# Token-major V for two head groups at a time: 512 columns per matmul, k blocks outermost, five PSUM banks open

## The chip, the cores and the metric

The kernel runs on one core of one Trainium2 chip. The metric is device time in microseconds (us). Five engines work side by side and wait for each other through semaphores: TensorE (PE, with its weight loads shown apart as PEld), VectorE (DVE), ScalarE (ACT), GpSimd (POOL) and SyncE (SP), which here does nothing but start DMAs. TensorE multiplies a stationary operand of 128 columns, which a weight load puts into the array, with a moving operand that streams past it, and writes sums into PSUM, eight banks of 128 x 512 fp32.

## The reference

One layer of a decoder: 512 prompt tokens and 64 sample tokens (8 sequences of 8) share all weights. All tokens are projected by one wide matrix; two of the three branches of the mixer have a "V" in it:

```python
(q_g, k_g, v_g, r_g, a_lr, u_pool, q_a, k_a, v_a,
 g_a, g_b, g_c) = jnp.split(xn @ w_in, _split_points(), axis=-1)
v_g = v_g.reshape(bsz, t_len, GLA_HEADS, GLA_DV)          # 4 heads x 256: gated linear attention
o_g, gla_new = gla_chunked(q_g, k_g, v_g, log_a, s0)
...
v_a = v_a.reshape(bsz, t_len, ATT_HEADS, ATT_HEAD_DIM)    # 12 heads x 64: dilated attention
for gi, (win, dil) in enumerate(ATT_GROUPS):              # (128,1), (512,4), (2048,16)
    hs = slice(gi * ATT_HEADS_PER_GROUP, (gi + 1) * ATT_HEADS_PER_GROUP)
    qh, kh, vh = q_a[:, :, hs], k_a[:, :, hs], v_a[:, :, hs]
```

A group of the dilated attention has 4 heads x 64 = 256 columns of V. In groups 1 and 2 a query reads keys 4 and 16 tokens apart, so the kernel holds the tokens of these two groups in strided order (token t, t+4, t+8, ...).

## The kernel before

Everything is fp32 in value. To multiply at TensorE's fast rate, each operand is split into a rounded high part and the rest (`xh`, `xl` for the normalised tokens; `wh`, `wl` for weights), and a product is three matmuls: high by high, low by high, high by low. A weight "chunk" is 1,024 fp32 per partition, loaded by one DMA of SP into one of three buffers `wr`; it is cut into two pieces of 512 by a copy on ACT (line 148, `wh`) and a subtraction on DVE (line 150, `wl`), each tag with four buffers. The list `chunks` fixes the order of loading; `fetch(i)` cuts chunks i and i+1 and loads i+2 and i+3.

Most projections are made by `gemm` (line 231): the weights are stationary, tokens are the moving operand in two parts of 256 to 320 columns, and the result has channels on partitions. V is needed with tokens on partitions, so `token_major` (lines 400 to 432, its matmuls on line 423) turns the roles round: a block of 128 tokens of `xh` or `xl` is stationary, and 256 columns of weights stream. It goes through the token blocks one after another (block 4, the 64 sample tokens packed as high and low parts into `xsp`, first; then 0, 1, 2, 3), for each through the eight blocks of k; blocks 2 and 3 are done in two halves of k. That is 4 x 8 x 3 + 8 x 2 = 112 matmuls. Blocks 0 and 1 share a bank. It is called seven times: for each of the four heads h of the gated linear attention (lines 535 to 538), and for the attention groups 2, 1, 0 (line 1011). For groups 2 and 1 the stationary block is `xh[:, n, t::4]`: 128 tokens that lie four fp32 apart.

PSUM has a pool `g` of three banks (`big`) and a pool of five (`small`, of which one bears the tag `h`). Evacuations: line 427 (ACT) and 428 (DVE) add the two halves of the sample block, 430 and 432 (ACT) copy the token blocks.

The order in which instructions stand on each engine is not that of the code: a scheduler builds it at compile time from its own estimate of durations, and pools decide when a buffer is free. On the chip each engine then runs its list strictly in order. So dense matmuls of `gemm` and V stand between the small steps of the two attentions, as filler for their waits. Steps that the prediction names: in the gated linear attention of head h the norm's sums (line 682), the transposes of `kp` (581), `kp` itself (POOL, 568 and 569), and the scans of the forget gate (DVE, 502 and 503); in the dilated attention, which runs one prompt unit and some steps of a sample unit in turn, the products with cached keys and values (910, 893, 898, 965; the cache arrives in four buffers `kv`), the softmax of a sample (819, 946, 948, 949), the values of the prompt (849, 857), the rescaling (1084, 1086) and the last transposes (1092). The gates `gc` (line 1101) are 384 dense matmuls that follow the attention in the code, and stand between its steps in the order; the last 24 of them are held until line 1092 has run.

Of the kernel before, what the change touches and what calls it, by code (L numbers as in the profile page):

```python
# [9 lines left out]
F32 = mybir.dt.float32  # L10
# [3 lines left out]
OP = mybir.AluOpType  # L14
# [6 lines left out]
NP = 512  # L21
# [12 lines left out]
C_Q, C_K, C_V, C_R, C_LR, C_U = 0, 512, 1024, 2048, 3072, 3088  # L34
C_QA, C_KA, C_VA, C_GA, C_GB, C_GC = 4112, 4880, 5648, 6416, 7440, 8464
# [69 lines left out]
def hybrid_step(ctx: ExitStack, tc: tile.TileContext, I, O, at_a, at_b):  # L105
    nc = tc.nc
    V, S, G, T = nc.vector, nc.scalar, nc.gpsimd, nc.tensor
# [8 lines left out]
    def big():  # L116
        return psg.tile([128, 512], F32, tag="g", name="g")
# [6 lines left out]
    def small():  # L124
        turn[0] += 1
        if turn[0] % 5 == 0 and not apart[0]:
            return held()
        return pss.tile([128, 512], F32, tag="s", name="s", bufs=4)
# [13 lines left out]
    chunks = []  # L142
# [51 lines left out]
    for b in range(8):  # L194
        for which in range(2):
            for g in (2, 1, 0):
                src = I[KEYS[g][which]][0, b].rearrange("t h e -> t (h e)")
# [14 lines left out]
    def plan(name, c0, cols=128, r0=0, kt=8, plain=True):  # L212
        chunks.append(Chunk(rows(name, c0, cols, r0, kt), kt, cols, plain))
        return len(chunks) - 1

    def fetch(i):
        for n in range(i, min(i + 2, len(chunks))):
            chunks[n].split()
        for n in range(i + 2, min(i + 4, len(chunks))):
            if chunks[n].plain:  # L220
                chunks[n].load()
# [51 lines left out]
    P = {}  # L273
    GROUPS = (2, 1, 0)
    for h in range(4):
        P["k", h] = [plan("w_in", C_K + 128 * h)]
        P["q", h] = [plan("w_in", C_Q + 128 * h)]
        P["v", h] = [plan("w_in", C_V + 256 * h, 256, r, 4) for r in (0, 4)]
        for d in range(2):
            P["r", 2 * h + d] = [plan("w_in", C_R + 256 * h + 128 * d)]  # L280
    def plan_u(n):
# [25 lines left out]
    for g in GROUPS:  # L307
        for p in range(2):
            P["qa", 2 * g + p] = [plan("w_in", C_QA + 256 * g + 128 * p)]
            P["ka", 2 * g + p] = [plan("w_in", C_KA + 256 * g + 128 * p)]  # L310
        P["va", g] = [plan("w_in", C_VA + 256 * g, 256, r, 4) for r in (0, 4)]
    for m in range(8):
        P["gc", m] = [plan("w_in", C_GC + 128 * m)]
    for m in range(8):
# [14 lines left out]
    xh = xpool.tile([128, 8, NT], F32R, tag="xh", name="xh")  # L329
    xl = xpool.tile([128, 8, NT], F32R, tag="xl", name="xl")  # L330
# [41 lines left out]
    for t in range(5):  # L372
        n = 128 if t < 4 else 64
# [26 lines left out]
    def token_major(ids, order, out_p, out_s, tmp, xsp):  # L400

        fetch(ids[0])
        fetch(ids[1])
        ps = {4: big(), 0: big()}
        ps[1] = ps[0]
        for ts, ns in (((4,), range(8)), ((0,), range(8)), ((1,), range(8)), ((2, 3), range(4)), ((2, 3), range(4, 8))):
            for t in ts:
                if t not in ps:
                    ps[t] = big()
                c = 256 if t == 1 else 0  # L410
                dst = ps[t][:, c:c + 256]
                sel = slice(128 * t, 128 * t + 128) if order == 1 else slice(t, NP, 4)
                for n in ns:
                    wh, wl = chunks[ids[n // 4]].wide(n % 4)
                    if t < 4:
                        lh, ll = xh[:, n, sel], xl[:, n, sel]
                        seq = ((lh, wh), (ll, wh), (lh, wl))
                    else:
                        seq = ((xsp[:, n, :], wh), (xsp[:, n, :], wl))
                    for j, (a, b) in enumerate(seq):  # L420
                        first = t == 2 and n == 4 and j == 0
                        with tc.issue_after(mm.ins) if first else nullcontext():
                            mm = T.matmul(dst, a, b, start=(n == 0 and j == 0), stop=(n == 7 and j == len(seq) - 1))  # L423
                if ns[-1] < 7:
                    continue
                if t == 4:
                    S.copy(tmp, ps[4][64:128, :256])
                    V.tensor_tensor(out_s, ps[4][:64, :256], tmp, op=OP.add)  # L428
                elif t == 1:
                    S.copy(out_p[:, 0:2].rearrange("p b c -> p (b c)"), ps[1])  # L430
                elif t > 1:
                    S.copy(out_p[:, t, :], dst)


    xs_cm, xs_pool = open_pool("xs", "left")
    xsp = packed_sample(xs_pool)
# [85 lines left out]
    for h in range(4):  # L522
# [5 lines left out]
        for nm, dst, sc in (("k", kT, 1.0), ("q", qT, 128.0 ** -0.5)):  # L528
            if h:
                gemm(P[nm, h], XH, XL, lambda ps, t0, t1: S.mul(dst[:, t0:t1], ps, sc))  # L530
            else:
                for x, ps, a, b in kq0:
                    if x == nm:
                        S.mul(dst[:, a:b], ps, sc)
        vt = gl.tile([128, 4, 256], F32, tag="vt", name="vt", bufs=2)
        vs = gl.tile([64, 256], F32, tag="vs", name="vs", bufs=2)
        vtmp = gl.tile([64, 256], F32, tag="vtmp", name="vtmp", bufs=1)
        token_major(P["v", h], 1, vt, vs, vtmp, xsp)
        nc.sync.dma_start(sg, I["state_gla"][0, :, h].rearrange("b k v -> k b v"))

        bp, bs = views(bb[h])
# [450 lines left out]
    for g in GROUPS:  # L992
        W = WIN[g]
        load_bias(g)
        qT = ap.tile([128, 2, NP], F32, tag="aq", name="aq", bufs=2)
        kT = ap.tile([128, 2, NP], F32, tag="ak", name="ak", bufs=2)
        vt = ap.tile([128, 4, 256], F32, tag="av", name="av", bufs=2)
        vtmp = ap.tile([64, 256], F32, tag="avt", name="avt", bufs=1)
        for p in range(2):
            for nm, dst, dsts, sc in (("qa", qT, qs, 0.125), ("ka", kT, ksn, 1.0)):  # L1000
                def evac(ps, t0, t1):
                    if g == 0:
                        S.mul(dst[:, p, t0:t0 + 256], ps[:, :256], sc)
                    else:
                        S.mul(dst[:, p, :].rearrange("p (r i) -> p r i", r=4)[:, :, t0 // 4:t0 // 4 + 64],
                              ps[:, :256].rearrange("p (i r) -> p r i", r=4), sc)
                    if t0:
                        S.mul(dsts[:, 2 * g + p, :], ps[:, 256:], sc)

                gemm(P[nm, 2 * g + p], XH, XL, evac, SPLIT)  # L1010
        token_major(P["va", g], 1 if g == 0 else 4, vt, vsn[g], vtmp, xsp)
        if g == 2:
            pt = small()
            for p in range(2):
                qd = sa.tile([128, 2, 64], F32, tag="qd", name="qd", bufs=1)
                for d in range(2):
                    V.tensor_copy(qd[:, d, :], qs[:, 4 + p, :])
                T.transpose(pt[:, 128 * p:128 * p + 128], qd.rearrange("p d n -> p (d n)"), ident)
            qhl = sa.tile([128, 256], F32R, tag="qhl", name="qhl")
            S.copy(qhl, pt[:, :256])  # L1020
            V.tensor_tensor(qhl[64:128], pt[64:128, :256], qhl[64:128].bitcast(F32), op=OP.subtract)
            sel = sa.tile([128, 64], F32R, tag="sel", name="sel")
            V.tensor_tensor(sel, ident[:, 0:64], ident[:, 64:128], op=OP.add)

        for _ in prompt_units(g, qT, kT, vt):
            for _ in range(STEPS[g]):
                next(samples, None)
        if g == 0:
            for _ in samples:
                pass  # L1030

        ko = sa.tile([128, 4, 256], F32, tag="kv", name="ko", bufs=4)
        for t in range(4):
            if g == 0 and t < 3:
                continue
            pk = small()
            for p in range(2):
                T.transpose(pk[:, 128 * p:128 * p + 128], kT[:, p, 128 * t:128 * t + 128], ident)
            S.copy(ko[:, t, :], pk[:, :256])
        kos = ap.tile([64, 256], F32, tag="avt", name="kos", bufs=1)  # L1040
        pk = small()
        for p in range(2):
            T.transpose(pk[:64, 128 * p:128 * p + 128], ksn[:, 2 * g + p, :], ident)
        S.copy(kos, pk[:64, :256])
        for n, tok, smp in ((K_OUT[g], ko, kos), (V_OUT[g], vt, vsn[g])):
            o = O[n][0, 0].rearrange("t h e -> t (h e)")
            if g == 0:
                nc.sync.dma_start(o, tok[:, 3, :])
            else:
                nc.sync.dma_start(o.rearrange("(i r) f -> i r f", r=4), tok)  # L1050
            for b in range(8):
                nc.sync.dma_start(O[n + 1][0, b].rearrange("t h e -> t (h e)")[W - 8:W], smp[8 * b:8 * b + 8, :])
        if g == 1:
            nc.sync.dma_start(scr.rearrange("(i r) c -> i r c", r=4), stp.rearrange("p r g m h -> p r (g m h)"))
            nc.sync.dma_start(nat[:, :, 1:3].rearrange("p t g m h -> p t (g m h)"), scr.rearrange("(t p) c -> p t c", p=128))
# [461 lines left out]
```

## Time and profile before

| what | before |
|---|---|
| time, median of 3 runs | 1308.93 us (1308.63 to 1310.06) |
| the profiled execution's own time | 1308.33 us |
| its span, first to last instruction | 1306.3 us |
| mean granted TensorE clock | 0.998 |
| matmuls on line 423, by the page's groups of 224 (prompt blocks) | 71.2, 71.1 and 70.8 us, 318, 318 and 316 ns each |
| first and last start of line 423 | 35.8 and 684.1 us |

A matmul's duration in the trace has a modelled end, and the next one starts before it is over; what a matmul costs the engine is therefore read from the distance between two starts. A timeline row gives start, duration, engine, line, operation, out<-in, sizes (stationary, then moving) and count; in brackets stands how long the engine was idle before it and who released it.

### The profile page before, as it was taken

To read this page: it belongs to the slowest core of one execution; us is meant where nothing else is said; L and a number is where in the kernel's file an instruction comes from. 1 tells how busy PE (TensorE), PEld (TensorE's weight loads), DVE (VectorE), ACT (ScalarE), POOL (GpSimd) and SP (SyncE) were. 2 spreads that over 40 slices of the span, in tenths; PEclk is the share of its full clock that TensorE was granted. 3 is DMA by queue.
4 is the path that set the end of the run, shared out by engine and by line. 5 is a ranking of instruction groups with operands and counts; after the bars stand their busy time and mean duration, and the time that the engine had idled before them with its cause. 6 is when DMAs were issued, how large, how long until landed. Compare 5 with 4: busy or idle time off the path is not lost.

```text
span 1306.3 us, 24224 instructions
## 1 busy us (share of the span) xinstructions
PE 1276.7 (98%) x9699; PEld 1226.0 (94%) x9699; DVE 685.9 (53%) x1294; ACT 572.0 (44%) x1262; POOL 250.0 (19%) x400
## 2 busy tenths in 40 slices
PE   8899999999999999999999999999999999999996
PEld 6899999999999999998988879999999999999996
DVE  5855554333462323172733357545897878873233
ACT  6654553544332222243543334444456656662333
POOL 4321212013420222041311101022231222200000
PEclk9999999999999999999999999999999999999999
DMA  7242432376483677355766432563556656544423
GB/s 221 66 125 62 146 113 74 98 232 192 154 257 93 216 239 245 110 168 174 219 195 211 141 103 78 161 216 114 161 151 151 141 132 146 125 113 141 137 77 117
DMA packets 225484, 196.39 MB, mean 150 GB/s; under 512 B 8444, under 2 KB 216937, under 8 KB 224596
## 3 DMA queue, kind: packets, MB, share of 16 engines
q1 hardware_dynamic: 218682, 142.28, 37.3%
q0 software_dynamic: 6688, 52.57, 13.3%
q8 instruction: 76, 1.25, 0.4%
q14 instruction: 36, 0.29, 0.1%
q10 hardware_dynamic: 2, 0.00, 0.0%
HBM read 175.52 MB, written 54.27 MB: 176 GB/s over the span
## 4 chain that ended last, share of the span: by engine, by line
PE 82%; issue 5%; DVE 5%; ACT 4%; DMA 3%; SPq 1%; POOL 0%; POOLq 0%; ACTq 0%; DVEq 0%
PE g L231 43%; PE g L1431 8%; PE g L423 7%; PE g L1274 6%; PE s L1274 3%; PE s L1431 2%; DMA wr<-wr 1%; DVE wl L150 1%; PE h L1274 1%; PE s L833 1%; PE s L231 1%; PE h L965 1%; PE s L910 1%; PE s L893 1%; ACT wh L148 1%
## 5 line engine op out<-in xcount | busy, mean ns | idle before, releaser
L150 DVE TENSOR_TENSOR wl<-wr,wh 128x512 fp32r<-128x512 f32 (+2 forms) x286 | 202.0, 709 | 324.2 <-ACT wh L148 318.2
L231 PE MATMUL g<-xh,wh 128*128 128x288 f32 (+2 forms) x1120 | 333.6, 298 | 3.1 <-DVE ae L1320 1.6
L231 PE MATMUL g<-xh,wl 128*128 128x288 f32 (+2 forms) x1120 | 333.9, 298 | 0.5 <-DVE wl L150 0.5
L231 PE MATMUL g<-xl,wh 128*128 128x288 f32 (+2 forms) x1120 | 332.1, 296 | 0.0
L148 ACT CAST wh<-wr 128x512 fp32r<-128x512 f32 (+2 forms) x290 | 174.9, 607 | 339.1 <-PE g L231 232.0
L231 PEld LDWEIGHTS g<-xh,wh 128*128 128x128 f32 x1120 | 211.1, 189 | 5.8 <-issue 2.5
L231 PEld LDWEIGHTS g<-xh,wl 128*128 128x128 f32 x1120 | 211.0, 188 | 2.8 <-issue 1.4
L231 PEld LDWEIGHTS g<-xl,wh 128*128 128x128 f32 x1120 | 211.0, 188 | 1.6 <-issue 1.3
L1234 DVE TENSOR_TENSOR wl<-wr,wh 128x512 fp32r<-128x512 f32 x119 | 81.2, 707 | 22.9 <-ACT wh L1233 22.6
L1233 ACT CAST wh<-wr 128x512 fp32r<-128x512 f32 x119 | 70.2, 619 | 46.3 <-DVE wr L1225 23.7
L423 PE MATMUL g<-wh,xh 128*128 128x256 f32 x224 | 71.2, 318 | 2.8 <-DVE vs L428 2.8
L1431 PE MATMUL g<-hh,wh 128*128 128x288 f32 (+2 forms) x286 | 71.3, 297 | 0.2 <-ACT hh L1245 0.2
L1431 PE MATMUL g<-hh,wl 128*128 128x288 f32 (+2 forms) x286 | 71.2, 297 | 0.0
L423 PE MATMUL g<-wh,xl 128*128 128x256 f32 x224 | 71.1, 318 | 0.0
L423 PE MATMUL g<-wl,xh 128*128 128x256 f32 x224 | 70.8, 316 | 0.0
L1431 PE MATMUL g<-hl,wh 128*128 128x288 f32 (+2 forms) x286 | 70.7, 296 | 0.0
L1274 PE MATMUL g<-xh_t,wh 128*128 128x288 f32 x204 | 60.6, 297 | 0.5 <-DVE h L1367 0.3
L1274 PE MATMUL g<-xh_t,wl 128*128 128x288 f32 x204 | 60.3, 296 | 0.0
L1274 PE MATMUL g<-xl_t,wh 128*128 128x288 f32 x204 | 59.9, 294 | 0.0
L423 PEld LDWEIGHTS g<-wh,xh 128*128 128x128 f32 x224 | 51.6, 230 | 4.2 <-DVE vs L428 3.0
L423 PEld LDWEIGHTS g<-wh,xl 128*128 128x128 f32 x224 | 51.6, 230 | 1.6 <-issue 1.6
L423 PEld LDWEIGHTS g<-wl,xh 128*128 128x128 f32 x224 | 51.7, 231 | 0.0
(520 smaller groups left out, 2984.6 us busy)
## 6 DMA issues: line engine op xcount, KB each, us to landing
wr<-in_w_in_dram SPq DMA_DIRECT2D x74, 512.0 KB
wr<-in_ffn_w_up_dram SPq DMA_DIRECT2D x44, 512.0 KB
out_dram<-in_cache_k_w_dram POOLq DMA_DIRECT2D x8, 2040.0 KB, 9.6
out_dram<-in_cache_v_w_dram POOLq DMA_DIRECT2D x8, 2040.0 KB, 9.7
kv<-in_cache_k_w_dram SPq DMA_DIRECT2D x26, 512.0 KB
kv<-in_cache_v_w_dram SPq DMA_DIRECT2D x26, 512.0 KB
wr<-wr POOLq DMA_DIRECT2D x34, 256.0 KB, 3.6
wr<-in_ffn_w_down_dram SPq DMA_DIRECT2D x18, 448.0 KB
```

The source lines that it names most:

```text
L148: S.copy(hi[:, :n], src)
L150: return hi, lo, E.tensor_tensor(lo[:, :n], src, hi[:, :n].bitcast(F32), op=OP.subtract)
L231: T.matmul(ps[:, :t1 - t0], a, b(n)[:, t0:t1], start=(n == 0 and j == 0), stop=(n == len(ks) - 1 and j == 2))
L423: mm = T.matmul(dst, a, b, start=(n == 0 and j == 0), stop=(n == 7 and j == len(seq) - 1))
L833: T.matmul(sps[hh][:, nk * n:nk * n + nk], qT[r, p, 128 * t:128 * t + 128], kT[r, p, k0:k0 + nk], start=True, stop=True)
L893: T.transpose(pk[:, 128 * n:128 * n + 128], kt[:, 2 * half + n // 2, 128 * (n % 2):128 * (n % 2) + 128], ident)
L910: T.matmul(pq[:, 256 * n:256 * n + 256], sel[:, tok:tok + 1].to_broadcast([128, 128]), qhl, start=True, stop=True)
L965: T.matmul(po[32 * b:32 * b + 32, :256], pz[:, 32 * b:32 * b + 32], vt[:, b, :], start=False, stop=(r == NR[g] - 1))
L1233: S.copy(hi, src)
L1234: V.tensor_tensor(lo, src, f32(hi), op=OP.subtract)
L1274: T.matmul(ps, a[:, 128 * k:128 * k + 128], b[:, k, :], start=start and k == 0 and j == 0, stop=k == 3 and j == 2, skip_group_check=True)
L1431: T.matmul(q[:, :t1 - t0], a, b[n][:, t0:t1], start=(n == 0 and j == 0), stop=(n == NF - 1 and j == 2))
```

## The change

`token_major_pair` makes V for 512 columns at once: for heads 0 and 1 (during head 0), for heads 2 and 3 (during head 2), and for attention groups 1 and 2 together (during group 2). Group 0 keeps `token_major`. The k blocks are the outer loop, the five token blocks the inner one, so all five sums are open at the same time: three banks of `g`, two of `small`. One chunk now holds 2 k blocks of 512 columns in place of 4 of 256.

```diff
+        if h % 2 == 0:
+            P["v", h] = [plan("w_in", C_V + 256 * h, 512, r, 2) for r in (0, 2, 4, 6)]
-        P["v", h] = [plan("w_in", C_V + 256 * h, 256, r, 4) for r in (0, 4)]
...
+        if g == 2:
+            P["va", g] = [plan("w_in", C_VA + 256, 512, r, 2) for r in (0, 2, 4, 6)]
+        if g == 0:
+            P["va", g] = [plan("w_in", C_VA, 256, r, 4) for r in (0, 4)]
-        P["va", g] = [plan("w_in", C_VA + 256 * g, 256, r, 4) for r in (0, 4)]
...
+    def token_major_pair(ids, order, outs, xsp):
+        ps = {4: big(), 0: big(), 1: big(), 2: small(), 3: small()}
+        for n in range(8):
+            if n % 2 == 0:
+                fetch(ids[n // 2])
+            wh, wl = chunks[ids[n // 2]].wide(n % 2)
+            for t in ps:
+                if t < 4:
+                    sel = slice(128 * t, 128 * t + 128) if order == 1 else slice(t, NP, 4)
+                    lh, ll = xh[:, n, sel], xl[:, n, sel]
+                    seq = ((lh, wh), (ll, wh), (lh, wl))
+                else:
+                    seq = ((xsp[:, n, :], wh), (xsp[:, n, :], wl))
+                for j, (a, b) in enumerate(seq):
+                    T.matmul(ps[t], a, b, start=(n == 0 and j == 0), stop=(n == 7 and j == len(seq) - 1))
+        for t in ps:
+            for x, (out_p, out_s) in enumerate(outs):
+                src = ps[t][:, 256 * x:256 * x + 256]
+                if t < 4:
+                    S.copy(out_p[:, t, :], src)
+                else:
+                    S.copy(out_s, src[64:128])
+                    V.tensor_tensor(out_s, src[:64], out_s, op=OP.add)
...
-        token_major(P["v", h], 1, vt, vs, vtmp, xsp)
+        if h % 2 == 0:
+            pairs = [(gl.tile([128, 4, 256], F32, tag="vt", name="vt", bufs=3),
+                      gl.tile([64, 256], F32, tag="vs", name="vs", bufs=2)) for _ in range(2)]
+            token_major_pair(P["v", h], 1, pairs, xsp)
+        vt, vs = pairs[h % 2]
...
-        token_major(P["va", g], 1 if g == 0 else 4, vt, vsn[g], vtmp, xsp)
+        if g == 2:
+            token_major_pair(P["va", g], 4, [(vts[x], vsn[x]) for x in (1, 2)], xsp)
+        if g == 0:
+            token_major(P["va", g], 1, vt, vsn[g], ap.tile([64, 256], F32, tag="avt", name="avt", bufs=1), xsp)
```

The lines from 435 on stand 30 to 35 lines lower in the changed file (the norm's sums are on line 713, `kp`'s transposes on 612, the last transposes on 1127).

Where it moves instructions, first on TensorE at the first V, head 0. The rows name moving and stationary operand after the arrow; `g` and `s` are banks of the two pools, and the numbers tell tiles apart. Before:

```order
L423 MATMUL g_546<-wh_358,xsp_260 128x256
L423 MATMUL g_546<-wl_360,xsp_260 128x256
...
L423 MATMUL g_546<-wh_362,xsp_260 128x256
L423 MATMUL g_546<-wl_364,xsp_260 128x256
...
L423 MATMUL g_547<-wh_358,xh_79 128x256
L423 MATMUL g_547<-wh_358,xl_80 128x256
L423 MATMUL g_547<-wl_360,xh_79 128x256
```

After:

```order
L454 MATMUL g_527<-wh_358,xsp_260 128x512
L454 MATMUL g_527<-wl_360,xsp_260 128x512
L454 MATMUL g_528<-wh_358,xh_79 128x512
L454 MATMUL g_528<-wh_358,xl_80 128x512
L454 MATMUL g_528<-wl_360,xh_79 128x512
L454 MATMUL s_530<-wh_358,xh_79 128x512
L454 MATMUL s_530<-wh_358,xl_80 128x512
L454 MATMUL s_530<-wl_360,xh_79 128x512
L454 MATMUL s_531<-wh_358,xh_79 128x512
L454 MATMUL s_531<-wh_358,xl_80 128x512
L454 MATMUL s_531<-wl_360,xh_79 128x512
```

Before, the sample block went through several weight pieces (358, 362, ...) within its first few matmuls; now each piece serves all token blocks before the next one is touched. (Block 1, bank `g_529`, whose bank frees last, catches up behind the fourth piece.)

On VectorE at the same place: `bb` are the scans of the forget gate, `vs` the sample block's sum, `wl` the low parts of weights. Before, the fourth piece of V is `wl_532`, and no more are needed:

```order
L150 TENSOR_TENSOR wl_532<-wr_128,wh_530 128x512
L503 SCALAR_TENSOR_TENSOR bb0_303<-ca_72,zt_307 128x576
L503 SCALAR_TENSOR_TENSOR bb1_304<-ca_72,zt_307 128x576
...
L428 TENSOR_TENSOR vs_524<-g_546,vtmp_525 64x256
L503 SCALAR_TENSOR_TENSOR bb2_305<-ca_72,zt_307 128x576
L503 SCALAR_TENSOR_TENSOR bb3_306<-ca_72,zt_307 128x576
```

After, four of the eight pieces of V stand ahead of the scans (the last of them `wl_538`) and four behind them:

```order
L150 TENSOR_TENSOR wl_538<-wr_128,wh_536 128x512
L533 SCALAR_TENSOR_TENSOR bb0_303<-ca_72,zt_307 128x576
L533 SCALAR_TENSOR_TENSOR bb1_304<-ca_72,zt_307 128x576
...
L533 SCALAR_TENSOR_TENSOR bb2_305<-ca_72,zt_307 128x576
L533 SCALAR_TENSOR_TENSOR bb3_306<-ca_72,zt_307 128x576
L150 TENSOR_TENSOR wl_572<-wr_366,wh_570 128x512
L150 TENSOR_TENSOR wl_576<-wr_366,wh_574 128x512
L150 TENSOR_TENSOR wl_610<-wr_540,wh_608 128x512
```

The sum of the sample block, which stood between the scans, has moved behind all eight pieces; the pieces five to eight stand where the scans end.

On TensorE at the end of the dilated attention (`ss` is a sample's softmax, `ae` the rescaling, `kv` the cache), ahead of the last transposes. Before, 26, 17, 20, 22 and 2 dense matmuls of line 231 stand between the last steps; the end of that:

```order
L231 MATMUL g<-xh,wh 128x288
L948 MATMUL s<-ca,ss 128x128
L949 MATMUL s<-ca,ss 64x128
L1038 MATMUL s<-ca,ak 128x128 x2
L1043 MATMUL s<-ca,ksn 64x128 x2
L1084 MATMUL s<-ca,ae 128x128 x4
L231 MATMUL g<-xl,wh 128x288
L231 MATMUL g<-xh,wl 128x288
L956 MATMUL h<-vsn_5713,ptn 128x256
L965 MATMUL h<-kv,ptc 32x256 x4
```

After, 26 and then 2; behind these two the steps follow each other with no dense matmul between them, down to the last transposes:

```order
L231 MATMUL g<-xh,wl 128x288
L880 MATMUL s<-ca,as 128x128 x4
L987 MATMUL h<-vsn_5483,ptn 128x256
L996 MATMUL h<-kv,ptc 32x256 x4
L888 MATMUL s<-pts,av 64x128 x4
L970 MATMUL h<-ksn,qb 128x64 x2
L929 MATMUL h<-skT,qb 32x128 x8
L979 MATMUL s<-ca,ss 128x128
L980 MATMUL s<-ca,ss 64x128
L1073 MATMUL s<-ca,ak 128x128 x2
L1078 MATMUL s<-ca,ksn 64x128 x2
L1119 MATMUL s<-ca,ae 128x128 x4
```

So 59 dense matmuls that stood in this tail have moved ahead, to where V of group 1 stood between the steps of group 2's attention. In the same way, head 1 and head 3 of the gated linear attention have lost their V: between the norm's last sums of the head before (line 682, now 713) and the transposes of `kp` (581, now 612) of head 1 stood 53 dense matmuls and the 112 of V, and now stand 74 dense ones (as many ahead of head 3).

More of the change, by code (lines that the diff above doesn't have):

```diff
@@ L534, in hybrid_step @@
                         S.mul(dst[:, a:b], ps, sc)
-        vt = gl.tile([128, 4, 256], F32, tag="vt", name="vt", bufs=2)
-        vs = gl.tile([64, 256], F32, tag="vs", name="vs", bufs=2)
-        vtmp = gl.tile([64, 256], F32, tag="vtmp", name="vtmp", bufs=1)
-        token_major(P["v", h], 1, vt, vs, vtmp, xsp)
+        if h % 2 == 0:
[3 more added lines that the diff above has]
+        vt, vs = pairs[h % 2]
         nc.sync.dma_start(sg, I["state_gla"][0, :, h].rearrange("b k v -> k b v"))
@@ L996, in hybrid_step @@
         kT = ap.tile([128, 2, NP], F32, tag="ak", name="ak", bufs=2)
-        vt = ap.tile([128, 4, 256], F32, tag="av", name="av", bufs=2)
-        vtmp = ap.tile([64, 256], F32, tag="avt", name="avt", bufs=1)
+        if g != 1:
+            vts = {x: ap.tile([128, 4, 256], F32, tag="av", name="av", bufs=2) for x in ((1, 2) if g else (0,))}
+        vt = vts[g]
         for p in range(2):
```

## The prediction

> **What bounds the kernel now.** I read the page first: how much of the span TensorE is busy, and what the chain that ended last is made of.
>
> ```profile
> span 1306.3 us, 24224 instructions
> PE 1276.7 (98%) x9699; PEld 1226.0 (94%) x9699; DVE 685.9 (53%) x1294; ACT 572.0 (44%) x1262; POOL 250.0 (19%) x400
> PE 82%; issue 5%; DVE 5%; ACT 4%; DMA 3%; SPq 1%; POOL 0%; POOLq 0%; ACTq 0%; DVEq 0%
> ```
>
> TensorE is busy for 98% of the span and makes up 82% of the chain; every other engine has half its time free. So the time is what TensorE's instructions cost, plus its few stops, and I price the change by TensorE's starts. Then the windows of the dilated attention (busy us and count of PE, PEld, DVE, ACT, POOL; clock, DMA share, GB/s):
>
> ```profile
> 557.00:591.00 34.00, 34.00 (x272) 32.86 (x271) 25.61 (x61) 17.69 (x53) 13.83 (x17) 1.00 0.61 184
> 591.00:626.00 35.00, 35.00 (x226) 30.47 (x227) 5.84 (x18) 9.60 (x27) 3.54 (x8) 1.00 0.57 178
> 626.00:661.00 35.00, 35.00 (x285) 33.22 (x286) 25.11 (x62) 18.42 (x54) 11.86 (x13) 1.00 0.71 215
> 661.00:685.00 24.00, 23.85 (x224) 19.37 (x227) 6.12 (x22) 9.84 (x31) 3.56 (x8) 1.00 0.63 187
> ```
>
> Here too TensorE does not stop. But 591 to 626, where V of group 1 is the filler, has 226 matmuls in 35 us; 661 to 685, the same steps with V of group 0, has 224 in 24 us. The timeline says why. The first two rows are 23 starts apart, the next two 16, the next two 32, the last two 66:
>
> ```profile
> 32.40 0.31 PE L231 MATMUL g<-xh,wh 128*128 128x320 f32 x1
> 35.77 0.31 PE L231 MATMUL g<-xh,wl 128*128 128x320 f32 x1
> 54.34 0.30 PE L231 MATMUL g<-xh,wh 128*128 128x288 f32 x1
> 56.45 0.30 PE L231 MATMUL g<-xl,wh 128*128 128x288 f32 x1
> 49.20 0.28 PE L423 MATMUL g<-wh,xh 128*128 128x256 f32 x1
> 53.04 0.28 PE L423 MATMUL g<-wl,xh 128*128 128x256 f32 x1
> 541.01 0.40 PE L423 MATMUL g<-wh,xl 128*128 128x256 f32 x1
> 556.41 0.40 PE L423 MATMUL g<-wh,xl 128*128 128x256 f32 x1
> ```
>
> A matmul thus costs 0.1465 us at 320 columns, 0.132 at 288 and 0.120 at 256: 0.000415 us per column and 0.0138 besides. But with strided tokens stationary, 256 columns cost 0.2333. The weight loads show what is slow there:
>
> ```profile
> 533.27 0.19 PEld L423 LDWEIGHTS g<-wl,xsp 128*128 128x128 f32 x1
> 533.39 0.31 PEld L423 LDWEIGHTS g<-wh,xh 128*128 128x128 f32 x1
> 533.60 0.33 PEld L423 LDWEIGHTS g<-wh,xl 128*128 128x128 f32 x1
> ```
>
> The load itself takes 0.31 to 0.33 in place of 0.19, already on the first strided row, whose forerunner is contiguous; the matmul waits for it.
>
> **The change, part by part.** *Width, strided groups.* On the line of the three widths, 512 columns cost 0.120 + 256 x 0.000415 = 0.226. This is less than the 0.2333 of a strided load, so if loads go on running under the streaming, a strided matmul of 512 columns costs the same 0.2333. Before: 2 x (96 x 0.2333 + 16 x 0.120) = 48.6. After: 96 x 0.2333 + 16 x 0.226 = 26.0. That is **-22.6**.
>
> *Width, four heads.* Before 4 x 112 x 0.120 = 53.8, after 2 x 112 x 0.226 = 50.6: **-3.2**.
>
> The trace has no rounded matmul wider than 320 columns. The nearest of 512 is plain fp32 with one row:
>
> ```profile
> L368 PE MATMUL s<-grow,ones 1*128 1x512 f32 x4 | 3.7, 1089 | 2.2 <-DMA grow<-in_norm_g_dram 2.2
> ```
>
> Its 1.089 us is the upper end, 0.2333 or 0.226 the lower. I take the lower, since three rounded widths lie on one line and this row is another kind.
>
> *Stops of V.* Five stand in the timeline, all for weight pieces or a bank:
>
> ```profile
> 40.22 0.39 PE L423 MATMUL g<-wh,xsp 128*128 128x256 f32 x1 [0.54 <-ACT wh L148]
> 45.70 0.28 PE L423 MATMUL g<-wl,xh 128*128 128x256 f32 x1
> 48.74 0.39 PE L423 MATMUL g<-wh,xh 128*128 128x256 f32 x1 [2.75 <-DVE vs L428]
> 48.96 0.28 PE L423 MATMUL g<-wh,xl 128*128 128x256 f32 x1
> 94.97 0.39 PE L423 MATMUL g<-wl,xsp 128*128 128x256 f32 x1 [0.91 <-DVE wl L150]
> 148.07 0.38 PE L423 MATMUL g<-wl,xsp 128*128 128x256 f32 x1 [0.28 <-DVE wl L150]
> 199.51 0.39 PE L423 MATMUL g<-wl,xsp 128*128 128x256 f32 x1 [0.28 <-DVE wl L150]
> ```
>
> Idle is 4.76 in all; from start to start a stop costs some 0.27 more (45.70 to 48.74 is 3.04, then 0.22, against 2 x 0.120): 6.1. These waits exist because the sample block runs through all pieces within 2 us and because four sums share three banks. With k outermost a piece lasts 14 x 0.226 = 3.2 us. A new wait comes at the first pair: piece five is cut behind the scans.
>
> ```profile
> 35.92 0.28 PE L423 MATMUL g<-wh,xsp 128*128 128x256 f32 x1
> 48.28 0.41 DVE L428 TENSOR_TENSOR vs<-g,vtmp 64x256 f32<-64x256 f32 x1
> 48.61 2.59 DVE L503 TENSOR_TENSOR_SCAN bb<-ca,zt 128x576 f32<-128x576 f32 x2
> ```
>
> Without line 428 ahead of them the scans end near 50.9, and the cut adds 0.7: 51.6. TensorE has four pieces and nine matmuls with the fifth's high part: 35.92 + 65 x 0.226 = 50.6. One us of stop, and 0.5 for the pair of head 2: **-4.6**, at worst nothing (-6.1 to 0).
>
> *Evacuation.* The rows of the copies (ns: least, median, most):
>
> ```profile
> L430 ACT COPY vt<-g x4: 586/586/586, 49.0 to 203.7; 128x512 f32<-128x512 f32 x4
> L432 ACT COPY vt<-g x8: 361/369/373, 51.9 to 210.2; 128x256 f32<-128x256 f32 x8
> ```
>
> Per pair ACT now makes ten copies of at most 256 columns, 3.7 us; before, two V took some 3.4. The sample bank and blocks 0 and 1 are done 12, 9 and 6 matmuls ahead of the end, and ten small transposes and matmuls stand between V and the next `gemm`; I cost this at nothing, or one copy (0.4) per pair without that cover.
>
> *Heads 1 and 3, which lose their V as filler.* What stood under it, by head 1:
>
> ```profile
> 84.59 0.29 PE L682 MATMUL s<-sqr,onesr 128*128 128x288 f32 x1
> 92.05 0.92 POOL L569 COPY kp<-ddlast 128x256 f32<-128x256 f32 x1
> 106.35 0.60 PE L581 MATMUL h<-ca,kp 128*128 128x128 f32 x4
> ```
>
> `kp` is ready 8.4 us after the norm's last sums, and was used at 21.8. Now 74 dense matmuls of 0.132, 9.8 us, cover it, with 1.4 to spare. Behind line 581 wait all of the head's small matmuls and the next `gemm`. I take **+1.0** for both heads (0 to 4, the upper end being the spare gone and 2 us late each).
>
> *End of the attention.* 59 dense matmuls, 7.8 us, have left the tail:
>
> ```profile
> 763.81 0.66 PE L857 MATMUL s<-pts,av 128*64 128x128 f32 x8
> 772.73 0.66 PE L898 MATMUL h<-skT,qb 128*32 128x128 f32 x16
> 774.24 0.19 ACT L946 ACTIVATION_READ_ACCUMULATOR ss<-ss,smx 128x1 f32 x1
> 776.90 0.27 PE L948 MATMUL s<-ca,ss 128*128 128x128 f32 x1
> 783.24 0.52 PE L1092 MATMUL s<-ca,orow 128*128 128x128 f32 x3 [0.75 <-DVE orow L1089]
> ```
>
> The softmax between lines 898 and 948 takes 1.7 us and was covered; now about 1.3 of it is bare. The other waits down to line 1092 were bare before in part (0.75). From line 857 to 1092 were 19.4 us; less 7.8 leaves 11.6, and I take **+1.5** (0 to 5, the whole chain bare twice over).
>
> *Middle of the attention.* Cache loads and POOL's masks must follow a faster TensorE. The window 661 to 685 shows the same value steps beside contiguous V with 0.15 us of stop, so I expect little: **+1.5**. Upper end: 557 to 685 moved 184 x 34 + 178 x 35 + 215 x 35 + 187 x 24 = 24.5 MB in 128 us; if 215 GB/s were the ceiling it needs 114, and 128 less the 24.3 of V is 103.7: 10 at most. V takes 256 x 1,024 fp32 of weights with it, 1 MB or 4.9 us of that, so 6 is my end.
>
> Sum: -22.6 - 3.2 - 4.6 + 1.0 + 1.5 + 1.5 = -26.4, against the profiled execution's 1308.3 (0.6 below the median): **1281.9**.
>
> **A rule that speaks against it.** The Trainium skill, "TensorE: Matmul & The Clock Gate", "Part 3: Packing small matmuls — row/col tiling", says a weight load overlaps a running matmul only if the row groups differ. By that rule the pair of groups would save 2 in place of 22.6, as the first rival has it; the contiguous rows do not agree, since load and streaming share 0.120.
>
> **The rivals.** *No overlap.* A strided load and 512 columns follow each other: 0.2333 + 512 x 0.000415 = 0.446 each, 96 of them 42.8, the pair 46.4: 1302. For it: nothing here streams longer than a strided load. Against it: 256 contiguous columns alone stream for 0.106, so 0.120 leaves no room for a load in series. 3%.
>
> *The attention's own steps become the bound.* Bare tail 5, cache loads 6, heads 4, in place of 4.0: 1293. For it: gates as filler are spent earlier. Against it: the window 661 to 685. 20%.
>
> *Wide streaming is slow*, the one that ends slower: beyond 320 columns the rate falls. V costs 102.4 now; with the stops won and lost it breaks even at 0.307 per wide matmul. At half rate, 0.44, it is 336 x 0.44 = 147.8 (less 0.6 net): 1353. The only row of that width, line 368's, is for it; the line of three widths against. 3%.
>
> *Wide streaming is faster than the line.* At 0.131 a wide matmul, heads and sample rows would save 240 x 0.095 = 23 more, the strided ones nothing: 1259. 320 columns at 0.1465 speak against it: 1%. The Trainium skill, same page, "Back-to-back issue gap", gives such a sustained 131 ns for 512; no run here shows it.
>
> **How the numbers follow.** My forecast has 73%: it spans 1276.4 (the stops of V all gone, nothing new) to 1286.5 (none of them won). With most of the second rival the range is 1276.5 to 1292, about 8 in 10. Faster by over 0.2% (what a measurement of this kernel can tell from no change) 0.95, within it 0.02, slower 0.03.
>
> **What would show it.** Starts of strided matmuls with 512 columns 0.233 apart, contiguous ones 0.226. V 50.6 plus 26.0 us. The first pair stops once, near its fifth piece, for DVE; no stop for `vs`. Line 612 without a stop behind 74 dense matmuls; ahead of line 1127 two or three stops of 1 us. Wrong would be a distance of 0.4 between strided rows, stops of PE for `kv` or `pz` in the attention, or a late `kp`.

## The result, and the profile after

| | before | after |
|---|---|---|
| median (range) of 4 runs each, us | 1308.78 (1307.66 to 1310.06) | 1288.86 (1286.71 to 1289.93) |
| ratio, 95% interval | 1 | 0.9848 (0.9834 to 0.9861) |
| profiled execution, its span, us | 1308.33, 1306.3 | 1286.71, 1284.6 |

The changed kernel is 19.9 us faster, inside the range of 1276.5 to 1292.0 and 7.0 above the predicted 1281.9. The first lines of the page of the changed kernel:

```profile
span 1284.6 us, 23535 instructions
PE 1254.8 (98%) x9363; PEld 1193.8 (93%) x9363; DVE 684.9 (53%) x1294; ACT 572.7 (45%) x1268; POOL 246.8 (19%) x400
```

TensorE is still busy for 98%, with 336 matmuls fewer (9363 for 9699). Its timeline in V, first the heads' contiguous tokens, then the attention's strided ones:

```profile
36.05 0.40 PE L454 MATMUL g<-wh,xh 128*128 128x512 f32 x1
36.28 0.39 PE L454 MATMUL g<-wh,xl 128*128 128x512 f32 x1
...
538.46 0.40 PE L454 MATMUL g<-wl,xh 128*128 128x512 f32 x1
538.69 0.40 PE L454 MATMUL s<-wh,xh 128*128 128x512 f32 x1
```

Starts are 0.23 apart in both; over whole pairs the mean is 0.227 contiguous and 0.235 strided, as the line of three widths and the strided load had given (0.226, 0.233). The weight loads of the same place:

```profile
538.22 0.31 PEld L454 LDWEIGHTS g<-wl,xh 128*128 128x128 f32 x1
538.46 0.31 PEld L454 LDWEIGHTS s<-wh,xh 128*128 128x128 f32 x1
...
539.87 0.19 PEld L454 LDWEIGHTS g<-wh,xsp 128*128 128x128 f32 x1
```

A strided load still takes 0.31 and a contiguous one 0.19, but now 512 columns stream beside it. TensorE's stops that matter (in brackets the idle time and what ended it), from its timeline:

```profile
50.12 0.39 PE L454 MATMUL s<-wh,xl 128*128 128x512 f32 x1
52.76 0.50 PE L454 MATMUL g<-wl,xsp 128*128 128x512 f32 x1 [2.25 <-DVE wl L150]
...
106.73 1.16 PE L634 MATMUL s<-qe,ddref 128*128 128x128 f32 x8 [0.59 <-DVE qe L591]
...
265.16 0.32 PE L743 MATMUL s<-ca,stl 120*128 120x120 f32 x1 [3.04 <-DMA stl<-in_state_pool_dram]
...
756.97 0.33 PE L979 MATMUL s<-ca,ss 128*128 128x128 f32 x1 [1.15 <-ACT ss L977]
...
763.09 0.41 PE L1127 MATMUL s<-ca,orow 128*128 128x128 f32 x2 [0.75 <-DVE orow L1124]
```

The stop for `vs` (2.75) is gone, one at the fifth piece is there, and one at line 743 has grown. The same transpose in the kernel before:

```profile
268.99 0.32 PE L712 MATMUL s<-ca,stl 120*128 120x120 f32 x1 [1.36 <-DMA stl<-in_state_pool_dram]
```

The windows of the changed kernel on both sides of that stop (busy us and count of PE, PEld, DVE, ACT, POOL; clock, DMA share, GB/s) show a second loss:

```profile
258.00:265.20 7.20, 4.17 (x32) 3.96 (x31) 3.40 (x6) 2.80 (x8) 0.25 (x4) 1.00 0.64 166
265.20:276.00 10.80, 10.80 (x70) 10.78 (x71) 3.88 (x9) 4.04 (x13) 5.40 (x10) 0.84 0.73 255
```

Behind the stop the granted clock falls to a mean of 0.84: from 266.4 to 269.8 dense matmuls of 320 columns start 0.27 apart in place of 0.1465.

Where the time went, by the same landmarks of both timelines (start of the row in us):

| stretch, up to | before | after | lead won |
|---|---|---|---|
| first norm sum of head 3 | 252.77 | 247.28 | 5.5 |
| transpose of `stl` | 268.99 | 265.16 | -1.7 |
| 159 matmuls further on | 289.90 | 287.60 | -1.5 |
| first V of the attention | 532.55 | 530.26 | 0 |
| first transpose of `orow`, end of the attention | 783.24 | 763.09 | 17.9 |

Behind the attention the two run the same rows; the profiled execution of the changed kernel was 1.6 us shorter there (511.5 against 513.1 to the last row), and a second profile of it (below) was not (513.4). So the account is 5.5 won in the heads, 3.2 given back in the pool stage, 17.9 won in the attention: 20.2.

For the attention I add up TensorE's rows from each start to the next, by line (us):

| | V | `gemm` | scores | other steps | sum |
|---|---|---|---|---|---|
| before | 65.0 | 104.6 | 12.1 | 69.0 | 250.7 |
| after | 40.0 | 107.3 | 14.4 | 71.2 | 232.8 |

V lost 25.0. Some 2.7 of it is only renamed: where a small step follows a dense matmul it starts about 0.1 later, and the filler there is now `gemm` in place of V. A net 22.3 is left, and 4.4 came back in the steps.

### The profile page after: what moved, and what is told of

Its sections match the earlier page's. It is cut to its first block, busy times and chain, and to the rows that moved or that the text cites. A ratio compares the mean times of both kernels' runs of the same rounds, so it can differ in the third digit from the quotient of the medians.

```text
span 1284.6 us, 23535 instructions
## 1 busy us (share of the span) xinstructions
PE 1254.8 (98%) x9363; PEld 1193.8 (93%) x9363; DVE 684.9 (53%) x1294; ACT 572.7 (45%) x1268; POOL 246.8 (19%) x400
## 5 line engine op out<-in xcount | busy, mean ns | idle before, releaser
L1466 PEld LDWEIGHTS g<-hh,wh 128*128 128x128 f32 x286 | 49.0, 188 | 1.8 <-ACT hh L1280 1.0
L1466 PEld LDWEIGHTS g<-hl,wh 128*128 128x128 f32 x286 | 49.0, 188 | 0.4 <-DVE hl L1281 0.4
L1466 PEld LDWEIGHTS g<-hh,wl 128*128 128x128 f32 x286 | 49.2, 188 | 0.0
L1262 POOL DMA_DIRECT2D wr<-wr x34 | 29.3, 863 | 79.7 <-DVE wl L1269 55.3
L1309 PEld LDWEIGHTS g<-xh_t,wh 128*128 128x128 f32 x204 | 38.4, 188 | 0.3 <-ACT u L1394 0.3
L1309 PEld LDWEIGHTS g<-xl_t,wh 128*128 128x128 f32 x204 | 38.4, 188 | 0.0
```

The lines of the kernel that those rows point to most:

```text
L1262: nc.gpsimd.dma_start(out, x, accum_op=OP.add)
L1309: T.matmul(ps, a[:, 128 * k:128 * k + 128], b[:, k, :], start=start and k == 0 and j == 0, stop=k == 3 and j == 2, skip_group_check=True)
L1466: T.matmul(q[:, :t1 - t0], a, b[n][:, t0:t1], start=(n == 0 and j == 0), stop=(n == NF - 1 and j == 2))
```

## Experiments

Each kernel was timed beside the kernel before on the same chip; the ratio goes by that. "Attention" is the time from its first V to the first transpose of `orow` in the profile, 250.7 before and 232.8 after.

**Only the attention's pair.** The heads' V as before:

```diff
-        if h % 2 == 0:
-            P["v", h] = [plan("w_in", C_V + 256 * h, 512, r, 2) for r in (0, 2, 4, 6)]
+        P["v", h] = [plan("w_in", C_V + 256 * h, 256, r, 4) for r in (0, 4)]
...
+        token_major(P["v", h], 1, vt, vs, vtmp, xsp)
```

> The GLA heads are as before, only V of groups 1 and 2 is made as one pair. Theory W (a strided matmul costs its weight load of 0.233 us, and 512 columns fill that time): this part carries nearly all, -17.8 us as between 526 and 785 us of the two profiles, 1291 (1289.5 to 1293). Rival G (the pairs of the GLA heads carry a good part, -6.8 as the prediction had it): -13 to -15, 1294 to 1296. Also asked: without the GLA pairs the pool stage should wait for stl as before (1.4 us), not 3.0.

Measured 1292.58, ratio 0.9887 (0.9870 to 0.9903), attention 233.4, stop for `stl` 0.86. The attention part alone brings 15.3 us; the profiled execution was 1291.21. That lies with theory W and its 1289.5 to 1293, but the interval, 1290.9 to 1295.2, holds most of G's 1294 to 1296 too. What decides is the profile, in which the attention alone is 17.3 shorter, close to W's 17.8, and the next run, in which the heads' pairs alone bring nothing like G's 6.8. The stop is short without the heads' pairs.

**Only the heads' pairs.** The attention's two edits undone:

```diff
-            token_major_pair(P["va", g], 4, [(vts[x], vsn[x]) for x in (1, 2)], xsp)
+        token_major(P["va", g], 1 if g == 0 else 4, vt, vsn[g], vtmp, xsp)
...
```

> The attention is as before, only the heads' V is made in pairs. Prediction's sum for this part: 3.2 + 4.6 - 1.0 = -6.8, 1302. Theory P (some 5.5 us are won up to the norm of head 3, and half of it is lost at the pool stage, where TensorE stands for stl and its clock falls): -2.3, 1306.5 (1304.5 to 1307). Under P the wait of the transpose of stl is again near 3 us, with dense matmuls at twice their distance for some 3 us behind it.

Measured 1305.58, ratio 0.9980 (0.9969 to 0.9991): 2.3 to 2.6 us, as theory P has it, and not 6.8. The stop for `stl` was 2.32, but the clock stayed at 1.00 behind it, so that part of P did not show in this run.

**Narrow matmuls in the changed order.** Each 512-column matmul as two of 256, with the loop order, the five banks and the pairs kept:

```diff
-                    T.matmul(ps[t], a, b, start=(n == 0 and j == 0), stop=(n == 7 and j == len(seq) - 1))
+                    for c in (0, 256):
+                        T.matmul(ps[t][:, c:c + 256], a, b[:, c:c + 256], start=(n == 0 and j == 0 and c == 0),
+                                 stop=(n == 7 and j == len(seq) - 1 and c == 256))
```

> The changed kernel with each 512-column matmul of V as two of 256 columns, each with its own weight load; pieces, loop order, five open banks and pairs stay. Theory W: the strided rows cost 2 x 96 x 0.233 + 2 x 16 x 0.120 = 48.6 again and the heads' 53.8, so the time goes back by 22.6 + 3.2: 1308 to 1315. Rival L (the loop order with five banks is what gains, by the stops it removes): 1289 to 1294.

Measured 1309.97, ratio 1.0014 (1.0006 to 1.0023): the whole gain is gone. Theory W stands and L falls: the new order by itself gains nothing that can be seen. In the profile V of the attention costs 62.4 again (48.6 strided and 13.8 contiguous, as the prediction counted it), and the attention takes 255.2, 4.5 more than before with V rows as narrow: this is what the new order costs in the attention, seen apart from the width.

**Contiguous tokens, narrow.** The kernel before, V of groups 2 and 1 from contiguous columns. Their tokens then come in another order than the reference asks for, so this kernel and the next one serve for measuring alone:

```diff
-        token_major(P["va", g], 1 if g == 0 else 4, vt, vsn[g], vtmp, xsp)
+        token_major(P["va", g], 1, vt, vsn[g], vtmp, xsp)
```

> The kernel before, with V of groups 2 and 1 taken from contiguous tokens (columns 128 t to 128 t + 127) in place of every fourth token, so the tokens of these two groups are in another order. Theory W: 192 matmuls fall from 0.233 to 0.120, -21.8, and some of it is given back as in the changed kernel (4 to 5 us): 1287 to 1292, with 256 columns a row still. Rival S (the strided rows are slow for something other than their load, for example the stop of the filler between steps): within 3 us of 1308.8.

Measured 1286.55, ratio 0.9839 (0.9827 to 0.9852), just below the expected 1287 to 1292: 21.3 us of the 21.8, with hardly anything given back (attention 228.4; scores 12.1, other steps 68.7 and `gemm` 104.6 as before). So the strided load was what the old V paid for, and removing it without the pairs costs nothing elsewhere. Rival S falls.

**Contiguous tokens, wide.** The same in the changed kernel:

```diff
-            token_major_pair(P["va", g], 4, [(vts[x], vsn[x]) for x in (1, 2)], xsp)
+            token_major_pair(P["va", g], 1, [(vts[x], vsn[x]) for x in (1, 2)], xsp)
```

> The changed kernel with V of groups 2 and 1 from contiguous tokens, so the tokens of these two groups are in another order. Theory W with the load hidden under 512 columns: 96 rows fall from 0.235 to 0.227, -0.8 us, which the times can hardly tell: 1287.5 to 1289; from the first V to the end of the attention 232.3 in place of 233.1. If a strided load still delayed something that the distances don't show (the next row's load, the steps between), 3 us or more would be won: under 1286.

Measured 1286.76, ratio 0.9838 (0.9815 to 0.9861), below the expected 1287.5 to 1289 and above the rival's 1286, with an interval that holds both. The profile tells more: V 39.2 in place of 40.0, the attention 232.3 in place of 232.8. Beside 512 columns a strided load costs next to nothing; the 4 us by which this attention is longer than that with narrow contiguous rows belong to the pairing. The granted clock fell behind the stop for `stl` in this run too, where that stop was only 2.10, and also behind the stop at the fifth piece.

**The changed kernel again**, beside the next three:

> The changed kernel once more, so that the next three are compared with it on the same chip: 1288.9 (1286.5 to 1290.5). Both theories of the pool stage expect a stop of 2.3 to 3.1 us for stl; if the stop is under 2.7 us, the clock should stay at 1.00 behind it (the stop of 2.75 us in the kernel before and that of 2.32 us in the run with the GLA pairs alone left it there, that of 3.04 us did not).

Measured 1288.36, ratio 0.9846 (0.9829 to 0.9863). The stop was 2.29 and the clock behind it 1.00. That fits the expected bound of 2.7, but the run above, with 2.10 and a fallen clock, contradicts it, and so does this run itself: its clock fell behind the other stop, that of 2.25 at the fifth piece. The length of the stop alone does not decide; the last section shows what goes with a fall.

**Gates first.** Two gates (12 us of dense matmuls) ahead of the first pooled channels, and with them a third ahead of the second ones:

```diff
-    MIDDLE = (("ga", 0, 1), ("ga", 2, 3), ("u", 0), ("ga", 4, 5), ("u", 1), ("ga", 6), ...
+    MIDDLE = (("ga", 0, 1), ("ga", 2, 3), ("ga", 4, 5), ("u", 0), ("ga", 6), ("u", 1), ...
```

> Only the order of the stage behind the GLA heads differs: two gates ahead of the first pooled channels instead of behind them, so that 12 us more of dense matmuls stand between the issue of stl and its transpose. Theory P (TensorE's stop for stl, and the half clock behind it, took back 3 us of what the heads won): no stop there, clock 1.00, 3.0 to 4.6 us below the changed kernel, 1284.3 to 1286. Rival Q (the stage is bound by POOL's sums and mixes, the stop only moves to the next mix): within 1 us of the changed kernel, with a stop of TensorE of 2 to 4 us for pl or ph.

Measured 1283.95, ratio 0.9819 (0.9806 to 0.9832): 4.4 below the changed kernel on that chip, as theory P has it, though the two intervals still touch and the time is just below the expected 1284.3. The stop is gone and the clock is 1.00 throughout the stage; no stop for `pl` or `ph` takes its place, so Q falls.

**`stl` early.** The first load of `stl` is issued ahead of head 3, into a tile that nothing uses until later; the order of the stage stays:

```diff
+        if h == 3:
+            nc.sync.dma_start(stl0, I["state_pool"][0].rearrange("b t c -> (b t) c")[:, 0:256])
...
```

> The changed kernel with the first load of stl put ahead of head 3, into a tile that is unused until the attention; the order of gates and pooled channels stays. If the stop is for stl (issue to transpose 5.0 to 5.9 us in the runs with the GLA pairs at full width, 3.7 to 4.3 without), it goes: 2 to 3 us below the changed kernel, 1285.5 to 1286.5 and up to 1284 where the half clock goes with it. If TensorE stands for something else (its transpose of stl came 2 us after the burst of weights and stl had ended, and the instruction queue moved a packet inside that burst), a stop of about 2 us stays at the same place with no load of stl ahead of it, and the time stays at 1287.5 to 1289.

Measured 1284.73, ratio 0.9813 (0.9799 to 0.9826). TensorE's timeline of this kernel has the transpose far ahead and without a stop, and nothing in its old place:

```profile
256.23 0.27 PE L749 MATMUL s<-ca,fvec 120*128 120x120 f32 x1
```

With this load moved, the stop and the fall of the clock behind it are gone: the stop was for `stl`. (In this execution the clock fell once elsewhere, behind the stop at the fifth piece.) Its issue on SP's queue, before and after (start, us):

```profile
264.70 1.29 SPq L705 DMA_DIRECT2D stl<-in_state_pool_dram  x2
```

```profile
259.26 1.21 SPq L736 DMA_DIRECT2D stl<-in_state_pool_dram  x2
```

From issue to transpose were 4.3 us before and 5.9 after. In the runs whose heads have wide pairs it was 5.0 to 5.9, in the others 3.7 to 4.3. One thing goes with it: in the five runs with 5.0 to 5.9 the instruction queue moves a packet of 16 KB, for 0.95 to 1.24 us, between issue and landing, and in the four others it moves none there. Whether that delays the load was not tried, so why it lands later stays open.

**Scores held together.** The scheduler had split three of the eight score steps of groups 2 and 1 in two. Here a one-column matmul into the second bank goes first, and the four follow it:

```diff
+        if len(heads) == 2:
+            mm = T.matmul(sps[1][:, :1], qT[64:, 0, 128 * t:128 * t + 128], kT[64:, 0, k0:k0 + 1], start=True, stop=True)
...
+                with tc.issue_after(mm.ins) if mm else nullcontext():
+                    mm = T.matmul(sps[hh][:, nk * n:nk * n + nk], qT[r, p, 128 * t:128 * t + 128], kT[r, p, k0:k0 + nk],
+                                  start=True, stop=True)
```

> The four matmuls of a score step of groups 2 and 1 are held together by a one-column matmul into the second bank ahead of them. Theory T (three steps split in two pairs cost 0.65 us a pair, as much as a whole step): the rows of the scores fall from 14.35 us to 12.1 us and some 0.6 for the eight small ones, the time by 1.5 to 2. Rival U (the pairs cost the same either way, and the 2.3 us are waits of the bank): 14 us and more, the time within 0.5 us.

Measured 1286.43, ratio 0.9837 (0.9822 to 0.9851), 1.9 below the changed kernel, but the intervals overlap and the attention is no shorter (234.3), so the 1.9 can't be put down to the scores. Their rows sum to 14.2 us, which is what rival U gave and not theory T's 12.7. The rows show why. A step of four matmuls (x8: two records each) in TensorE's timeline of the kernel before, then one that the change has split, then a step held together:

```profile
571.63 0.72 PE L833 MATMUL s<-ak,aq 64*128 64x128 f32 x8
```

```profile
571.62 0.71 PE L864 MATMUL s<-ak,aq 64*128 64x128 f32 x4
...
572.60 0.71 PE L864 MATMUL s<-ak,aq 64*128 64x128 f32 x4
```

```profile
569.72 0.38 PE L863 MATMUL s<-ak,aq 64*128 64x1 f32 x2
...
570.66 0.71 PE L868 MATMUL s<-ak,aq 64*128 64x128 f32 x8
```

Half a step takes as long as a whole one (0.64 to the next row). The four use 64 rows of the array each, two the upper half and two the lower, and run side by side; the split puts the two of one half together, with nothing beside them. Three splits cost 3 x 0.64 = 1.9 of the 2.3 us that the scores grew. Theory T's mechanism is right (a step held together takes 0.64 again) and its expected gain was not had: the one-column rows cost 0.22 to 0.31 each, some 2 us for eight in place of the expected 0.6, and a cache load came late once (a stop of 1.07). Why the scheduler splits these three steps was not tried.

**All three together**, with the scans of heads 2 and 3 behind the cuts:

```diff
+            with tc.issue_after(chunks[P["v", 0][2]].cut_at.ins):
+                scans((2, 3))
...
```

> The changed kernel with the gates first, the scores together, and the scans of heads 2 and 3 behind the cuts of pieces five and six of the first pair of V. If the three losses are what was read from the trace (3.0 to 4.6 at stl, 1.7 at the scores, 2.4 at the fifth piece), they add up: 7.1 to 8.7 below the changed kernel, 1280.2 to 1281.8. If they only move, 1284 or more, with a new stop of over 2 us behind the first V or in the pool stage.

Measured 1282.32, ratio 0.9800 (0.9786 to 0.9815): 6.0 below the changed kernel and not 7.1 to 8.7. The stops at the fifth piece and for `stl` are gone; the attention is 2.6 longer (235.4), with two stops for cache loads (0.91 and 1.08) and the one-column rows.

**Gates and scans alone:**

> The changed kernel with the gates first and the scans of heads 2 and 3 behind the cuts, the score steps as the change leaves them. If the one-column matmuls cost the run with all three parts about 1.9 us (eight of 0.22 to 0.31) and the score steps held together gave back 1.7, this run is within 0.5 us of it, 1282 to 1282.8. If the two late cache loads of that run (stops of 0.91 and 1.08) come from the steps being held together, they are gone here and it is 1280.5 to 1281.5. The stop of 2.25 us at the fifth piece is gone in either case.

Measured 1281.60, ratio 0.9799 (0.9782 to 0.9816). No stop at the fifth piece, none for `stl`, none for a cache load, the attention at 232.8. The time lies between the two expected ranges: it is 0.7 below the run with all three parts, on another chip, and the times can't tell the two apart. The profile can, and it has what the second case expected, no late cache load. These two are the fastest kernels of the study, 6 to 7 us below the changed kernel, and their intervals don't overlap with its own.

## Why the prediction was right, and where its 7 us went

*Width of the strided groups, -22.6.* Right: against the narrow rows in the same order V fell from 62.4 to 40.0, -22.4. The experiments on it agree: narrow rows lose the gain, contiguous rows win it without the width, both together win nothing more. The rival of no overlap falls by the 0.235 between starts, and with it the rule of the Trainium skill, "TensorE: Matmul & The Clock Gate", "Part 3: Packing small matmuls — row/col tiling": here loads of 0.31 ran under matmuls that used all rows of the array. The two rivals on wide streaming fall by the 0.227.

*Width, four heads, -3.2.* Right: the two pairs without their stop took 51.0 (50.6 predicted).

*Stops of V, -4.6.* The mechanism was right, the size was not. The one stop came at the fifth piece, for DVE, behind the scans, but from 50.12 to 52.76 it cost 2.4, not 1.0; the 0.5 for the pair of head 2 did not come. DVE's timeline of the changed kernel:

```profile
46.54 0.64 DVE L580 TENSOR_TENSOR ddref<-bb 128x64 f32<-128x64 f32 x1
47.10 0.72 DVE L579 TENSOR_TENSOR ddlast<-bb 128x512 f32<-128x512 f32 x1
...
47.96 3.79 DVE L533 TENSOR_TENSOR_SCAN bb<-ca,zt 128x576 f32<-128x576 f32 x2
51.67 2.44 DVE L150 TENSOR_TENSOR wl<-wr,wh 128x512 fp32r<-128x512 f32 x3
```

The scans end at 51.7 and not at 50.9, with steps of head 0 ahead of them, and the cut follows. In three of the later runs (the changed kernel again, contiguous tokens wide, `stl` early) the clock fell behind this stop as well, which it did not here. V of the heads fell from 59.8 to 53.4, -6.4 for both terms together in place of -7.8.

*Evacuation, 0.* Right: no stop for a bank or for `vt` follows the pairs.

*Heads 1 and 3, +1.0.* The size was right, the reason was not: line 612 has no stop, so `kp` was in time; two stops of 0.59 and 0.58 came behind it, at line 634, for `qe`.

*End of the attention, +1.5.* Right: from the first of its value rows (line 888, 750.23) to 763.09 were 12.9 us against the 11.6 that the old tail had without its 59 dense matmuls, +1.2, of which 1.15 stands at the softmax that was named.

*Middle of the attention, +1.5.* Too small, and for another reason than the one weighed. The attention won 17.9; with 22.3 from the width and 1.2 in the tail, 3.2 are lost in the middle. Neither cache loads nor POOL's masks stop TensorE there. The windows of the changed kernel at the place of those I had quoted:

```profile
619.00:654.00 35.00, 35.00 (x286) 33.32 (x285) 23.71 (x61) 15.97 (x46) 10.83 (x14) 1.00 0.73 218
654.00:678.00 24.00, 24.00 (x215) 17.66 (x214) 7.11 (x18) 9.52 (x28) 3.60 (x8) 1.00 0.83 250
```

250 GB/s without a stop: 215 was no ceiling. The loss is in rows that TensorE executes, 2.3 of it in the scores, 1.9 by three split steps; the remaining 0.9 is spread over many steps and was not settled.

*What had no term.* The pool stage gave back 3.2: 1.7 more of stop for `stl` and 1.5 of lower clock behind it. I had followed the change to the heads' last sums and then gone on to the attention, because hardly an instruction of TensorE in between had moved. The rival in which the attention's steps become the bound (1293) came nearest to the time, but by its sum only: of its three parts, the tail and the heads stayed at the forecast's size. So it is partly luck that the range held: the measured 1288.86 lies above the 1276.4 to 1286.5 of the forecast itself, in the part that was added for that rival, and what brought it there had no term at all.

Of the 7.0 us, 3.2 are thus the pool stage, 1.4 the stop at the fifth piece and 1.7 the middle of the attention; the rest is within the spread of the runs (3.2 us from the fastest to the slowest).

## What to carry over

Price a matmul by the distance between starts, and ask which of weight load and streaming sets it: here a slow strided load was paid in full at 256 columns and disappeared behind 512. When the engine that bounds the kernel is made to arrive elsewhere at another time, read every wait that the profile already has behind that place, stages without an edit too; the cheapest gain of this study, about 4 us, lay in one of them. Matmuls that share the array by row halves were cheap here only while they were issued in alternation, so look whether a new order splits them.

## What the runs showed of the hardware

A stop of TensorE of 2 to 3 us is sometimes followed by 3.41 us at half clock. In the thirteen profiled executions this came behind the stop for `stl` of 3.04 and of 2.10, but not of 2.15, 2.29 or 2.32; behind the stop of 2.25 at the fifth piece in three of seven; and behind the stop of 2.75 for `vs` in two of three (both with the heads' V as before), though not in the kernel before itself. The traces' record of the clock shows what goes with it. Each fall came a whole number of 3.41 us after the clock's last change, 10 to 239 of them. Cut the time into such stretches, and what goes with a fall is how much of a stop lies in one of them. The changed kernel again shows both cases, its stop of 2.25 in the first window and most of that of 2.29 in the third (TensorE's busy time stands behind the window's length, the clock third from the end):

```profile
50.11:53.52 3.41, 1.28 (x6) 0.74 (x4) 3.41 (x4) 1.30 (x3) 3.33 (x3) 1.00 0.00 0
53.52:56.93 3.41, 3.29 (x8) 2.61 (x9) 2.90 (x6) 0.62 (x1) 0.33 (x1) 0.50 0.40 115
...
265.13:268.55 3.42, 1.73 (x14) 1.73 (x15) 0.00 (x0) 0.43 (x2) 0.96 (x1) 1.00 0.58 161
268.55:271.96 3.41, 3.41 (x26) 3.41 (x25) 2.01 (x5) 1.82 (x5) 1.80 (x5) 1.00 0.99 342
```

Half clock followed all seven stretches in which TensorE stood for 1.97 us or more. In all others it stood for 1.68 at most, and only two of these were followed by half clock, at 869 and 870 us in the two runs with contiguous tokens: they held no stop, but matmuls of a single column took 1.93 us of them. The same 1.93 in one stretch brought no fall in three other runs. This is read from executions as they came; no run moved a stop against the stretches on purpose.

The Trainium skill, "TensorE: Matmul & The Clock Gate", "Part 1: The HAM clock gate", tells of a free-running window of about 3.4 us. The 3.41 us and their whole multiples agree with it; its advice that only gaps beyond that length matter does not agree with the falls behind 2.10 to 3.04.

Rounded fp32 matmuls keep to one line from 256 to 512 columns (0.120, 0.132, 0.1465 and 0.227 between starts). And a stationary operand taken from every fourth column loads in 0.31 to 0.33 in place of 0.19, beside 256 and beside 512 columns alike.
